# A streaming encoder trunk: the first mixer's output maps summed beforehand, and one modulation part moved into the gate

## Chip, cores and metric

The kernel runs as one launch on one core of one Trainium2 chip. The metric is the device time of that launch in microseconds (us). The engines are TensorE (PE in the rows, its weight loads PEld), VectorE (DVE), ScalarE (ACT), GpSimd (POOL) and SyncE (SP), whose queue issues most of the DMA transfers.

## What is computed

Two layers over 512 tokens of 1024 channels, in float32. The first layer is a state-space mixer (S5) with a gated linear unit behind it and then a feed-forward part; the second is an attention layer and again a feed-forward part. Each part takes a shift, a scale and a gate from the condition vector c. Cut to what the change touches:

```python
c_act = silu(c)
shift1, scale1, gate1, shift2, scale2, gate2 = split(c_act @ ada_w[0] + ada_b[0], 6)
h = rms_norm(x, norm1_g[0]) * (1 + scale1) + shift1
# S5: 64 groups of 16 channels, a complex diagonal state of 64 per group
#   state[t] = A * state[t-1] + B u[t]
#   y = Re(C state) + d * h
g = gelu(y)
x = x + gate1 * g * sigmoid(g @ w_glu + b_glu)
h = rms_norm(x, norm2_g[0]) * (1 + scale2) + shift2
x = x + gate2 * swiglu(h)
```

`ada_w[0]` is 1024 x 6144; the kernel works off its six parts of 1024 columns one by one, and names them by their place in the result: 0 and 8 (shift1, scale1), 16 (gate1), 24 (shift2), 32 (scale2), 40 (gate2).

## The kernel before, in words

**The S5 stage (`s5`).** The 512 steps are cut into 64 chunks of 8. Within a chunk the output is a product with a matrix of kernels (`intra`, L786); across chunks the state is summed per chunk (`sums`, L749), turned into a real recurrence (`turned`, L758), scanned (`scan`, L779), turned back, and multiplied by output maps (`inter`, L798). The groups are worked in quarters q = 0 to 3 for sums, turned, scan and kernels, and in eighths for inputs, intra and inter. The inputs of a quarter's products come from:

- `vmap(q)` on GpSimd (L586): three maps `vv[q][:, 0..2]`, in six products of 128x512. Re(C A^r) is map 0 plus map 1, Im(C A^r) is map 0 plus map 2. Both `kernels(q)` and `inter` multiply by the maps as they stand, so each complex product costs four matmuls, for (state part, map) = (0,0), (0,1), (1,0), (1,2).
- `tables(q)` on GpSimd (L598): the turning tables, five operations of 128x512, used by both `turned(q, False)` and `turned(q, True)`.
- `kernels(q)` (L658): products in PSUM, a copy on ScalarE (L670), a write to DRAM (`kd`, L672) and eight reads back (`tt`, L674), which spread it out for `intra`.

The maps of quarters 2 and 3 lie in part on the place of the normed input `xn`, which `inputs` (L727) reads.

**The modulation parts (`ada_rows`, L280).** A part is eight tiles of 128x1024, loaded from the SP queue (L290) into a ring of four places, of which three are the ring `raw` that the weights use later. Four *pairs* of tiles (eight matmuls each, L301) build a row sum; *close* copies the row to `adrow` on ScalarE (L306), spreads it with eight small matmuls (L309) and adds the bias. `adrow` uses the two-place ring `t1`, which is also the ring of the helper tiles `m` of `turned`. The rest of the parts, from 40 on, are worked off on VectorE much later. Each pair sends off two more loads.

**The order.** The tensor work of the S5 stage is chained by hand with `do(...)`, in the order of the calls at L825 to L891; GpSimd's work is chained by `behind(...)`. Other engines' instructions take the order that the scheduler gives them. Most products of the stage share one PSUM bank (`ps`): inputs, kernels, the closes and the transposes of the outputs (L814).

**The gate (`glu`, L1036).** gelu's output is split into a high and a low part (`split`, L920), and each weight block (128 columns of 1024 rows) is loaded, cast to its high part on ScalarE (L904) and its rest computed on VectorE (L164). Two blocks are multiplied at full width, then six at half width twice, as `outputs` (L998) says; after each half the next norm is started by `between`. `later` and `tick` (L119 to L125) put steps between matmuls by an estimated clock, in microseconds.

Of the kernel before, what the change touches and what calls it, by code (L numbers as in the profile page):

```python
# [11 lines left out]
F32 = mybir.dt.float32  # L12
# [3 lines left out]
ALU = mybir.AluOpType  # L16
# [39 lines left out]
class Trunk:  # L56
# [222 lines left out]

    def ada_rows(self, jobs, place):  # L280

# [10 lines left out]
        def pair(n, i):  # L292
            if i == 0:
                self.rows_acc = self.ps("ac")
            ks = (2 * i, 2 * i + 1)
            ws = [tiles.pop((n, k)) for k in ks]

            last = None
            for j in (3, 2, 1, 0):
                with self.after(last):  # L300
                    last = nc.tensor.matmul(self.rows_acc[32 * j:32 * j + 32], lhsT=self.csil[:, ks[j // 2]:ks[j // 2] + 1].to_broadcast([P, 32]),  # L301
                                            rhs=ws[j // 2][:, j % 2 * 512:j % 2 * 512 + 512], start=(i == 0), stop=(i == 3)).ins

        def close(at):
            row = self.tmp.tile([P, 512], F32, tag="t1", name=self.name("adrow"))
            nc.scalar.copy(out=row, in_=self.rows_acc)  # L306
            pt = self.ps()[:, 0:8]
            for m in range(4):
                nc.tensor.matmul(pt[:, 2 * m:2 * m + 2], lhsT=row[:, m * P:(m + 1) * P], rhs=self.rows, start=True, stop=True)  # L309
            cols = lambda t: t[:, at:at + 8].rearrange("a (h m) -> a m h", h=2)  # L310
            if at < 16:
                v.tensor_tensor(out=cols(self.mod), in0=pt.rearrange("a (m h) -> a m h", h=2), in1=cols(self.adab), op=ALU.add)
                return
            col = self.cst([P, 8], name="adcol")
            nc.scalar.copy(out=col, in_=pt)
            self.put_off.append(lambda: v.tensor_tensor(out=cols(self.mod), in0=col.rearrange("a (m h) -> a m h", h=2),
                                                        in1=cols(self.adab), op=ALU.add))

# [89 lines left out]
    def s5(self, ada):  # L408
# [4 lines left out]
        with ExitStack() as es:  # L413
# [172 lines left out]
            def vmap(q):  # L586
# [5 lines left out]
                return last  # L592


            turns = [[sp.tile([P, 8, 64], F32, tag=t, name=t) for t in ("tc", "ts")],
# [202 lines left out]
            def inter(q):  # L798
                for j in range(4):
                    gp = q * 4 + j  # L800
                    for n, (i, m) in enumerate(((0, 0), (0, 1), (1, 0), (1, 2))):
                        for b in range(2):
                            bp = slice(b * 64, b * 64 + 64)
                            self.last_mm = nc.tensor.matmul(py[q][bp, j * P:(j + 1) * P], lhsT=sb[q // 2 % 2][bp, i, gp % 8],  # L804
                                                            rhs=vv[gp // 8][bp, m, gp % 8].rearrange("a r p -> a (r p)"),
                                                            start=False, stop=(n == 3 and j == 3)).ins
                nc.scalar.copy(out=yt.rearrange("a i (g p) -> a g i p", p=16)[:, q % 2 * 4:q % 2 * 4 + 4],
                               in_=py[q].rearrange("a (g i p) -> a g i p", i=8, p=16))
                if q % 2:
                    ft = q // 2  # L810
# [9 lines left out]
            def behind(fn, q):  # L820
                nonlocal turn
                with wait(turn):
                    turn = fn(q)
# [9 lines left out]
            do(inputs, 3)  # L833
            pair()
            do(sums, 0)
# [5 lines left out]
            do(inputs, 5)  # L841
            pair()
            do(inputs, 6)
            pair()
            do(inputs, 7)
            do(kernels, 1)
            behind(vmap, 2)
            behind(tables, 2)
            pair()
# [4 lines left out]
            turned(0, True)  # L854
            behind(vmap, 3)
            behind(tables, 3)
            scan(1)
            do(sums, 2)
            do(inter, 0)
            pair()  # L860
            do(kernels, 2)
# [4 lines left out]
            turned(1, True)  # L866
            do(sums, 3)
            pair()
            do(inter, 2)
            scan(2)  # L870
            do(kernels, 3)
            do(intra, 3)
            pair()
# [8 lines left out]
            do(inter, 4)  # L882
            pair()
            do(inter, 5)
# [151 lines left out]
    def glu(self, between):  # L1036
# [15 lines left out]
        def blocks(m):  # L1052
            dst = [self.at(32 + 8 * m + 4 * i, [P, KT, P], F32R) for i in range(2)] if m < 2 else None
            return [self.wblock(self.io["s5_w_glu"][0], 0, KT, m * P, P, dst)]

# [512 lines left out]
    def run(self):  # L1568
        io, v, g = self.io, self.nc.vector, self.nc.gpsimd
        self.setup()  # L1570
        a0, a1, kv = io["ada_w"][0], io["ada_w"][1], io["kv_ada_w"]
        first = [(a0, at * P, at) for at in (0, 8, 16, 24, 32)]
        halves = lambda src, col, at, n: [(src, (col + 4 * i) * P, at + 4 * i, 4) for i in range(n)]
        later = halves(a0, 40, 40, 2) + halves(kv, 0, 96, 4) + halves(a1, 0, 48, 10)
        self.s5(first)
        self.banks(ps=6, st=2)
        self.wring = self.ctx.enter_context(self.tc.tile_pool(name="wring", bufs=4, reuse_waits="tile"))
        self.glu(self.ffn_in(0))
        self.dump("x1", self.xT)
# [37 lines left out]
```

## Time and profile before

| | us |
|---|---|
| median of 3 runs | 1234.67 |
| lowest, highest | 1229.35, 1234.99 |
| the profiled execution | 1233.43 |
| its span, first to last instruction | 1231.6 |
| S5 stage, up to the gate's first matmul | 175.4 |

How to read it: the profiled execution is one run, with the hardware's own record of each instruction; what is read of it below is its trace. "Busy" counts what an engine executes, "idle before" how long it had stood when an instruction began, and an arrow names who released it. PEclk (or the granted clock) is TensorE's clock as a share of its full speed. A matmul row can stand for two halves of a float32 product, so `inter`'s 32 products are 64 rows.

### The profile page before, as it was taken

To read this page: it belongs to the slowest core of one execution; us is meant where nothing else is said; L and a number is where in the kernel's file an instruction comes from. 1 tells how busy PE (TensorE), PEld (TensorE's weight loads), DVE (VectorE), ACT (ScalarE), POOL (GpSimd) and SP (SyncE) were. 2 spreads that over 40 slices of the span, in tenths; PEclk is the share of its full clock that TensorE was granted. 3 is DMA by queue.
4 is the path that set the end of the run, shared out by engine and by line. 5 is a ranking of instruction groups with operands and counts; after the bars stand their busy time and mean duration, and the time that the engine had idled before them with its cause. 6 is when DMAs were issued, how large, how long until landed. Compare 5 with 4: busy or idle time off the path is not lost.

```text
span 1231.6 us, 18830 instructions
## 1 busy us (share of the span) xinstructions
PE 1150.9 (93%) x7286; PEld 972.6 (79%) x7286; DVE 751.9 (61%) x1472; ACT 492.2 (40%) x914; POOL 133.7 (11%) x175
## 2 busy tenths in 40 slices
PE   5786879899999999999988888999999999999998
PEld 2555679888777777779987767889987888888888
DVE  8863347679788952565769899958752333232233
ACT  4641145343222232224567767834422223222222
POOL 5954000000000000000033242000000000000000
PEclk7897989899999999999998999999999999999999
DMA  9498834458878852455511121037443232323333
GB/s 273 176 258 145 180 86 139 119 147 261 258 249 259 270 172 85 134 157 155 153 41 31 35 69 35 1 92 209 137 131 100 86 103 86 102 78 103 111 115 100
DMA packets 230074, 167.53 MB, mean 136 GB/s; under 512 B 9776, under 2 KB 204256, under 8 KB 229984
## 3 DMA queue, kind: packets, MB, share of 16 engines
q1 hardware_dynamic: 208904, 128.47, 37.4%
q10 hardware_dynamic: 21080, 37.85, 9.2%
q8 instruction: 57, 0.93, 0.3%
q14 instruction: 33, 0.27, 0.1%
HBM read 163.21 MB, written 3.08 MB: 135 GB/s over the span
## 4 chain that ended last, share of the span: by engine, by line
PE 84%; DVE 8%; DMA 3%; ACT 3%; issue 1%; POOLq 0%; SPq 0%; DVEq 0%; ACTq 0%
PE ps L915 24%; PE ps L916 24%; PE ps L917 24%; PE ad L804 2%; PE ps L146 1%; PE ac L301 1%; DMA adaw<-in_ada_w 1%; DMA a<-in_x 1%; DVE a L923 1%; PE po L916 1%; PE zz L754 1%; DVE a L158 1%; DVE a L161 1%; DVE mn L1520 1%; PE po L917 1%
## 5 line engine op out<-in xcount | busy, mean ns | idle before, releaser
L916 PE MATMUL ps<-a,wh 128*128 128x512 f32 (+1 forms) x1406 | 493.7, 353 | 0.8 <-DVE a L989 0.8
L915 PE MATMUL ps<-a,wh 128*128 128x512 f32 (+1 forms) x1406 | 490.9, 354 | 3.5 <-ACT a L988 3.5
L917 PE MATMUL ps<-a,wl 128*128 128x512 f32 (+1 forms) x1406 | 494.1, 353 | 0.0
L904 ACT CAST wh<-raw 128x1024 fp32r<-128x1024 f32 (+1 forms) x179 | 182.6, 1022 | 503.7 <-PE ps L916 379.7
L164 DVE TENSOR_TENSOR wl<-raw,wh 128x1024 fp32r<-128x1024 f32 x173 | 207.1, 1199 | 193.9 <-ACT wh L904 190.2
L915 PEld LDWEIGHTS ps<-a,wh 128*128 128x128 f32 x1406 | 263.1, 189 | 44.0 <-ACT a L988 4.5
L916 PEld LDWEIGHTS ps<-a,wh 128*128 128x128 f32 x1406 | 265.4, 189 | 40.5 <-DVE a L989 1.1
L917 PEld LDWEIGHTS ps<-a,wl 128*128 128x128 f32 x1406 | 265.5, 189 | 39.6
L350 DVE SCALAR_TENSOR_TENSOR acc<-a,csil,acc 128x512 f32<-128x512 f32 x126 | 94.4, 749 | 31.0 <-DMA a<-in_ada_w 22.2
L1106 DVE TENSOR_TENSOR si<-si,ps 128x512 f32<-128x512 f32 x44 | 30.1, 684 | 81.0 <-PE ps L917 78.2
L146 PE MATMUL ps<-ident,a 128*128 128x128 f32 (+1 forms) x304 | 46.5, 295 | 17.4 <-DVE a L1447 4.8
L164 POOL TENSOR_TENSOR a<-raw,a 128x768 fp32r<-128x768 f32 (+1 forms) x2 | 4.6, 2309 | 506.3 <-ACT a L904 506.3
L146 PEld LDWEIGHTS ps<-ident,a 128*128 128x128 f32 (+1 forms) x304 | 37.4, 144 | 24.3 <-POOL a L158 6.1
L995 DVE SCALAR_TENSOR_TENSOR xT<-ps,mod,xT 128x256 f32<-128x256 f32 (+1 forms) x35 | 20.4, 582 | 45.8 <-PE ps L917 45.5
L1521 ACT ACTIVATE a<-ps,mn 128x128 f32<-128x128 f32 (+1 forms) x64 | 34.5, 546 | 13.3 <-DVE mn L1520 13.0
L915 PE MATMUL ps<-wh,a 128*128 128x288 f32 (+3 forms) x100 | 33.4, 336 | 1.8 <-ACT a L1521 1.3
L301 PE MATMUL ac<-adaw,csil 128*32 128x512 f32 x128 | 21.8, 708 | 13.7 <-DMA adaw<-in_ada_w 13.2
L916 PE MATMUL ps<-a,a 128*128 128x256 f32 (+2 forms) x108 | 33.4, 311 | 0.0
L915 PE MATMUL ps<-a,a 128*128 128x256 f32 (+2 forms) x108 | 33.1, 313 | 0.0
L917 PE MATMUL ps<-a,a 128*128 128x256 f32 (+2 forms) x108 | 32.8, 310 | 0.0
L917 PE MATMUL ps<-wh,a 128*128 128x288 f32 (+3 forms) x100 | 32.8, 329 | 0.0
L916 PE MATMUL ps<-wl,a 128*128 128x288 f32 (+3 forms) x100 | 32.6, 328 | 0.0
(317 smaller groups left out, 1473.1 us busy)
## 6 DMA issues: line engine op xcount, KB each, us to landing
a<-in_ada_w ACTq DMA_DIRECT2D x112, 256.0 KB, 4.3
raw<-in_ffn_w_gate SPq DMA_DIRECT2D x44, 512.0 KB, 3.9
raw<-in_ffn_w_up SPq DMA_DIRECT2D x44, 512.0 KB, 5.5
raw<-in_ffn_w_down SPq DMA_DIRECT2D x42, 512.0 KB, 4.2
adaw<-in_ada_w SPq DMA_DIRECT2D x32, 512.0 KB, 6.9
a<-in_kv_ada_w ACTq DMA_DIRECT2D x32, 256.0 KB, 4.3
raw<-in_ffn_w_down SPq DMA_DIRECT2D x21, 384.0 KB, 3.5
raw<-in_s_w_glu SPq DMA_DIRECT2D x14, 512.0 KB, 4.4
```

The source lines that it names most:

```text
L146: self.nc.tensor.transpose(out=out, in_=in_, identity=ident)
L164: eng.tensor_tensor(out=out, in0=a, in1=b, op=ALU.subtract)
L301: last = nc.tensor.matmul(self.rows_acc[32 * j:32 * j + 32], lhsT=self.csil[:, ks[j // 2]:ks[j // 2] + 1].to_broadcast([P, 32]), rhs=ws[j ...
L350: v.scalar_tensor_tensor(out=acc, in0=x, scalar=self.csil[:, k:k + 1], in1=acc, op0=ALU.mult, op1=ALU.add)
L804: self.last_mm = nc.tensor.matmul(py[q][bp, j * P:(j + 1) * P], lhsT=sb[q // 2 % 2][bp, i, gp % 8], rhs=vv[gp // 8][bp, m, gp % 8].rearran ...
L904: nc.scalar.copy(out=flat(wh), in_=flat(raw))
L915: mm(out, lhsT=lhs[0], rhs=rhs[0], start=start, stop=False)
L916: mm(out, lhsT=lhs[0], rhs=rhs[1], start=False, stop=False)
L917: self.last_mm = mm(out, lhsT=lhs[1], rhs=rhs[0], start=False, stop=stop).ins
L995: self.nc.vector.scalar_tensor_tensor(out=self.xT[:, m, sl], in0=src, scalar=gate[:, m:m + 1], in1=self.xT[:, m, sl], op0=ALU.mult, op1=AL ...
L1106: nc.vector.tensor_tensor(out=t, in0=t, in1=pp[i][1], op=ALU.mult)
L1521: nc.scalar.activation(out=p[:, self.OFF[t]:self.OFF[t] + w], in_=pt, func=AF.Exp, scale=-1.0, bias=mn[:, t:t + 1], accum_out=su[:, t:t + 1])
```

## The change

Three edits go together.

- `added(q)` on GpSimd: map 0 is added to maps 1 and 2 in place, in four operations of 128x512, once `kernels(q)` has read the maps. `inter` then takes two matmuls, (0,1) and (1,2), in place of four.
- The part at 32 leaves the S5 stage. Its loads and steps are put into the gate by the estimated clock: load k at 1.5 k, the pairs and the close from 13.0 on, 2.9 apart. Its tiles go to places of the arena that the S5 stage leaves. In the S5 stage five calls of `pair()` go, and the row tile of a close gets a place of its own (`sums`) in place of one of `t1`.
- Orders: GpSimd does tables 2, added 0, maps 2, maps 3, added 1, tables 3, added 2, added 3 (before: maps 2, tables 2, maps 3, tables 3). The casts of the gate's first weight block wait on ScalarE for the copy of inter 6, the others for that of inter 7, and their VectorE halves for the last operation of `turned(3, True)`.

```diff
-            row = self.tmp.tile([P, 512], F32, tag="t1", name=self.name("adrow"))
+            row = self.tmp.tile([P, 512], F32, **({"tag": "sums", "bufs": 1} if rows == "ac" else {"tag": "t1"}), name=self.name("adrow"))
...
-            if at < 16:
+            if at not in (16, 24):
...
+            def added(q):
+                for i in (1, 2):
+                    for h in (0, 4):
+                        x = vv[q][:, :, h:h + 4]
+                        last = g.tensor_tensor(out=x[:, i], in0=x[:, i], in1=x[:, 0], op=ALU.add)
+                return last
...
-                    for n, (i, m) in enumerate(((0, 0), (0, 1), (1, 0), (1, 2))):
+                    for n, (i, m) in enumerate(((0, 1), (1, 2))):
...
             do(inputs, 3)
-            pair()
             do(sums, 0)
...
-            pair()
             do(inputs, 6)
-            pair()
             do(inputs, 7)
+            behind(tables, 2)
+            behind(added, 0)
             do(kernels, 1)
             behind(vmap, 2)
-            behind(tables, 2)
+            behind(vmap, 3)
             pair()
...
             turned(0, True)
-            behind(vmap, 3)
+            behind(added, 1)
             behind(tables, 3)
             scan(1)
             do(sums, 2)
             do(inter, 0)
-            pair()
             do(kernels, 2)
...
             do(sums, 3)
+            behind(added, 2)
             pair()
             do(inter, 2)
             scan(2)
             do(kernels, 3)
+            behind(added, 3)
...
             do(inter, 4)
-            pair()
             do(inter, 5)
...
-            return [self.wblock(self.io["s5_w_glu"][0], 0, KT, m * P, P, dst)]
+            with self.tc.issue_after(self.s5_last.ins), self.tc.issue_after((self.s5_out if m else self.s5_late).ins):
+                return [self.wblock(self.io["s5_w_glu"][0], 0, KT, m * P, P, dst)]
...
-        first = [(a0, at * P, at) for at in (0, 8, 16, 24, 32)]
+        first = [(a0, at * P, at) for at in (0, 8, 16, 24)]
...
+        load, steps = self.ada_rows([(a0, 32 * P, 32)], lambda n, k: self.at(80 + 4 * k, [P, 1024]), "st", "st")
+        for k in range(KT):
+            self.later(1.5 * k, lambda k=k: load(0, k))
+        for i, f in enumerate(steps):
+            self.later(13.0 + 2.9 * i, f)
         self.glu(self.ffn_in(0))
```

## Rows read from the trace of the kernel before

**Rows 1.** The page, busy time of each engine over the whole span.
```profile
PE 1150.9 (93%) x7286; PEld 972.6 (79%) x7286; DVE 751.9 (61%) x1472; ACT 492.2 (40%) x914; POOL 133.7 (11%) x175
```
**Rows 2.** Windows: stretch, its length, busy of each engine, clock, DMA share, GB/s.
```profile
57.00:90.30 33.30, 27.78 (x415) 18.68 (x413) 21.38 (x33) 17.13 (x53) 18.53 (x16) 0.95 0.81 221
90.30:175.40 85.10, 63.44 (x965) 52.74 (x961) 34.11 (x49) 21.23 (x40) 17.12 (x14) 0.86 0.73 155
176.00:188.00 12.00, 12.00 (x61) 10.14 (x60) 2.74 (x4) 4.29 (x8) 0.00 (x0) 1.00 0.01 2
188.00:221.40 33.40, 33.34 (x282) 32.94 (x281) 26.24 (x53) 18.11 (x30) 0.00 (x0) 1.00 0.55 158
221.40:232.00 10.60, 7.54 (x39) 7.25 (x40) 10.35 (x21) 6.89 (x12) 0.00 (x0) 0.68 0.72 199
```
**Rows 3.** Matmul groups of 90.3 to 175.4: busy, mean ns, idle before.
```profile
L804 PE MATMUL ad<-a,a 64*64 64x128 f32 x512 | 30.2, 274 | 0.0
L301 PE MATMUL ac<-adaw,csil 128*32 128x512 f32 x44 | 7.8, 645 | 4.3 <-DMA adaw<-in_ada_w 4.3
L754 PE MATMUL zz<-a,a 128*64 128x64 f32 x128 | 5.8, 270 | 6.0 <-DVE a L776 6.0
L814 PE MATMUL ps<-ident,a 128*128 128x128 f32 x24 | 4.4, 311 | 9.9 <-ACT a L817 7.7 <-ACT a L807 2.2
L309 PE MATMUL ps<-rows,adrow 128*128 128x2 f32 x16 | 2.9, 304 | 0.7 <-ACT a L817 0.7
```
**Rows 4.** Timeline of TensorE in that stretch: start, length, what, idle before.
```profile
106.68 0.66 PE L814 MATMUL ps<-ident,a 128*128 128x128 f32 x4 [2.09 <-ACT a L817]
...
117.89 3.68 PE L754 MATMUL zz<-a,a 128*64 128x64 f32 x64 [6.04 <-DVE a L776]
...
145.48 1.92 PE L301 MATMUL ac<-adaw,csil 128*32 128x512 f32 x4 [4.27 <-DMA adaw<-in_ada_w]
147.33 4.40 PE L804 MATMUL ad<-a,a 64*64 64x128 f32 x64
...
162.66 1.12 PE L814 MATMUL ps<-ident,a 128*128 128x128 f32 x4 [4.91 <-ACT a L817]
```
**Rows 5.** Timeline of VectorE in the S5 stage.
```profile
64.28 2.68 DVE L161 TENSOR_TENSOR a<-a,sgu 128x512 f32<-128x512 f32 x2
...
80.38 0.68 DVE L161 TENSOR_TENSOR a<-a,sgu 128x512 f32<-128x512 f32 x1
...
87.78 0.67 DVE L164 TENSOR_TENSOR a<-zz,m 128x504 f32<-128x504 f32 x1
94.43 0.69 DVE L158 TENSOR_TENSOR m<-zz,a 128x512 f32<-128x512 f32 x1 [5.98 <-POOL a L610]
...
110.06 0.69 DVE L158 TENSOR_TENSOR m<-zz,a 128x512 f32<-128x512 f32 x1 [14.33 <-PE ps L309]
```
**Rows 6.** Timeline of ScalarE in the S5 stage.
```profile
87.32 0.61 ACT L756 COPY rr<-r 128x504 f32<-128x504 f32 x1 [3.24 <-DVE zz L781]
...
161.01 1.04 ACT L904 CAST wh<-raw 128x1024 fp32r<-128x1024 f32 x1 [3.96 <-DMA raw<-in_s_w_glu]
```
**Rows 7.** Timeline of GpSimd: an in-place add, and its last two waits and tables.
```profile
28.31 1.27 POOL L161 TENSOR_TENSOR a<-a,a 128x512 f32<-128x512 f32 x1
...
80.86 1.15 POOL L158 TENSOR_TENSOR a<-a,pw 128x512 f32<-128x512 f32 x1 [14.45 <-DMA tt<-kd]
...
106.55 1.26 POOL L610 TENSOR_TENSOR ts<-k,k 128x512 f32<-128x512 f32 x1
```
**Rows 8.** Timeline of the SP queue around kernels 1, issue times.
```profile
88.23 0.38 SPq L672 DMA_DIRECT2D kd<-a  x1
...
91.32 6.35 SPq L674 DMA_DIRECT2D a<-kd  x8
```
**Rows 9.** The line of the reads back (L674): issue to landing of one.
```profile
DMA to landing us min/median/max: 4.0/7.0/9.3
```

More of the change, by code (lines that the diff above doesn't have):

```diff
@@ L278, in vectors, with ada_rows @@
         self.kvag, self.qg = cols[:, 48:50], cols[:, 50:52]
-    def ada_rows(self, jobs, place):
+    def ada_rows(self, jobs, place, rows="ac", cols="ps"):
         nc, v = self.nc, self.nc.vector
@@ L293, in pair @@
             if i == 0:
-                self.rows_acc = self.ps("ac")
+                self.rows_acc = self.ps(rows)
             ks = (2 * i, 2 * i + 1)
@@ L304, in close @@
         def close(at):
-            row = self.tmp.tile([P, 512], F32, tag="t1", name=self.name("adrow"))
+            row = self.tmp.tile([P, 512], F32, **({"tag": "sums", "bufs": 1} if rows == "ac" else {"tag": "t1"}), name=self.name("adrow"))
             nc.scalar.copy(out=row, in_=self.rows_acc)
-            pt = self.ps()[:, 0:8]
+            pt = self.ps(cols)[:, 0:8]
             for m in range(4):
                 nc.tensor.matmul(pt[:, 2 * m:2 * m + 2], lhsT=row[:, m * P:(m + 1) * P], rhs=self.rows, start=True, stop=True)
-            cols = lambda t: t[:, at:at + 8].rearrange("a (h m) -> a m h", h=2)
-            if at < 16:
-                v.tensor_tensor(out=cols(self.mod), in0=pt.rearrange("a (m h) -> a m h", h=2), in1=cols(self.adab), op=ALU.add)
+            part = lambda t: t[:, at:at + 8].rearrange("a (h m) -> a m h", h=2)
+            if at not in (16, 24):
+                v.tensor_tensor(out=part(self.mod), in0=pt.rearrange("a (m h) -> a m h", h=2), in1=part(self.adab), op=ALU.add)
                 return
@@ L315, in close @@
             nc.scalar.copy(out=col, in_=pt)
-            self.put_off.append(lambda: v.tensor_tensor(out=cols(self.mod), in0=col.rearrange("a (m h) -> a m h", h=2),
-                                                        in1=cols(self.adab), op=ALU.add))
+            self.put_off.append(lambda: v.tensor_tensor(out=part(self.mod), in0=col.rearrange("a (m h) -> a m h", h=2),
+                                                        in1=part(self.adab), op=ALU.add))
         steps = []
@@ L805, in inter @@
                                                             rhs=vv[gp // 8][bp, m, gp % 8].rearrange("a r p -> a (r p)"),
-                                                            start=False, stop=(n == 3 and j == 3)).ins
-                nc.scalar.copy(out=yt.rearrange("a i (g p) -> a g i p", p=16)[:, q % 2 * 4:q % 2 * 4 + 4],
+                                                            start=False, stop=(n == 1 and j == 3)).ins
+                self.s5_out = nc.scalar.copy(out=yt.rearrange("a i (g p) -> a g i p", p=16)[:, q % 2 * 4:q % 2 * 4 + 4],
                                in_=py[q].rearrange("a (g i p) -> a g i p", i=8, p=16))
+                if q == 6:
+                    self.s5_late = self.s5_out
                 if q % 2:
```

## Prediction

> **What bounds the kernel now.** I read the page first: TensorE is busy 93% of the span [rows 1], so a change counts where it takes TensorE work away or lets it start sooner. Then the windows [rows 2], because an average hides the stages. From 176 us on TensorE is busy without a break at full clock (12.00 of 12.00, then 33.34 of 33.40), so what is put in there costs its whole length. In the stretch 90.3 to 175.4, the back half of the S5 stage, it is busy only 63.4 of 85.1 us at a granted clock of 0.86. That is where this change works. Then I took that stretch by groups [rows 3] to see what the busy time is made of, and by time [rows 4] to see what ends each wait. The waits in [rows 3] add up to 20.9 us (9.9, 6.0, 4.3, 0.7); 85.1 - 63.4 = 21.7 is all. Last I followed three of them on the other engines [rows 5, 6] and GpSimd's and the SP queue's own pace [rows 7 to 9].
>
> **A. From 57 to 90.3, up to sums 2.** Sums 2 needs the banks that `turned(0, True)` frees; its last operation runs at 87.78 [rows 5] and ends at 88.45, so the VectorE chain from sums 0 is the bound here and TensorE, with 27.8 of 33.3 us busy, follows. The change takes three pairs out of this stretch, one of them ahead of sums 0, which brings the chain forward by about 1 us (a pair is 7.8 us over 5.5 of them, at most 1.4, in [rows 3]); a bias add leaves VectorE. Against it: kernels 1 and its copy stay behind inputs 6 and 7 on ScalarE, and the close of part 16 now stands directly before sums 2. GpSimd now does tables 2 and added 0 here, where it stood idle for 14.45 us [rows 7], waiting really for the transposes of inputs 7, whose place maps 2 overwrite; tables 2 touch no such place.
>
> One thing speaks against more GpSimd work at this spot. The same VectorE add `a<-a,sgu`, two inputs in SBUF, took 1.34 us each at 64.28, when GpSimd was at work, and 0.68 at 80.38, when it stood idle [rows 5]. In the Trainium skill, the page "SBUF — State Buffer", section "Who interferes with whom", says that a VectorE instruction with two SBUF inputs contends with a GpSimd one that reads SBUF. The trace agrees, by that pair of rows. Here the one add of that kind left in the stretch (inputs 4) now falls beside added 0. By the pair of rows that is +0.66 us; without such contention it would be nothing. The `turned` operations take one input from PSUM. So I set sums 2 at 88.5 in place of 90.3: **-1.8** (ends -3.5, and +1.5 if ScalarE's queue delays kernels 1's copy as it does now, behind the `rr` copy that waits 3.24 us for a scan [rows 6]).
>
> **B. From sums 2 to the gate's first matmul, now 85.1 us.** Busy 63.4 [rows 2].
> - Inter: half of 512 rows, 30.2 us [rows 3], goes: -15.1.
> - One pair (7.8/5.5 = 1.4) and one close (2.9/2 = 1.45) fewer in this stretch: -2.9.
> - Half-clock losses behind waits that go. The 64 rows of sums 3 took 3.68 us behind a 6.04 us wait [rows 4] against 5.8 - 3.68 = 2.1 for those of sums 2 [rows 3]; half a pair took 1.92 against 0.7 and the inter behind it 4.40 against 30.2/8 = 3.8, behind 4.27 us; four transposes 1.12 against 0.66, behind 4.91. Together -3.9.
>
> That leaves 41.5 busy. Of the 21.7 us idle, these go:
> - 6.04 before sums 3. VectorE stood 14.33 us until 110.06 [rows 5] for a place in `t1` that the close's row held; with a place of its own that goes, and so do the 5.98 us for tables 2 at 94.43, now made before maps 2.
> - 4.27 for a row tile at 145.48: each pair now sits further behind the pair whose end sends off its loads.
> - 4.91 shrinks to the 0.75 of the other transposes: ScalarE held the gelu back behind a cast that waited 3.96 us for a weight [rows 6]; the casts now come after the last copies.
>
> So 21.7 - 14.5 = 7.2 idle stays, mostly the copy and gelu between transposes, with one table load (2.09 [rows 4]). What is late next is `tt`. From kd's issue at 88.23 [rows 8] to the last of eight reads landed it is 3.1 + 6.35 + 7.0 = 16.4 us [rows 8, 9]. After the change TensorE's own work between kernels 3 and intra 6 is intra 3 to 5, two pairs, a close, inter 3 to 5 at 1.9 and two rounds of transposes, about 17 us; for kernels 1 and intra 2 it is about the same. So this cover just holds; I add 2 us (0 to 8). GpSimd is not late. An in-place add is 1.27 us [rows 7], so `added` costs 4 x 1.27 = 5.1 and all four 20.3. From the end of tables 1 on (66.4, 14.45 before 80.86), tables 2 take it to 73.5, added 0 to 78.6, maps 2 and 3 from 80 to 92.5, added 1 to 97.6, tables 3 to 104.7, added 2 to 110, added 3 to 115 (now it ends at 107.8 [rows 7]). Inter 2, 4 and 6, which wait for added 1, 2 and 3, come up on TensorE near 105, 119 and 127, counted from 88.5 by the order of the calls and the lengths above.
> B becomes 41.5 + 7.2 + 2 = 50.7, which is **-34.4** (ends -39 and -22).
>
> **C. In the gate.** Four pairs and a close come into a stretch that is full: 4 x 1.2 (the pairs outside the slow one: (7.8 - 1.92)/5) + about 1 = 5.5 us, at most 4 x 1.4 + 1.45 = 7.1, all on the path. Their eight loads (4.2 MB) cost nothing where they fall, because the DMA share is 0.01 from 176 to 188 and 0.55 after [rows 2]; without that cover each would stand before a weight block. The casts of the first block now come late, which hides behind the last transposes, and the ring behind them starts emptier: +1.5 (0 to 8). Together **+7** (5 to 15). The steps that are chained to TensorE's estimated clock come before the first half ends, so the norm has scale2 in time.
>
> **D. Behind it.** At 221.4 to 232 TensorE is busy 7.5 of 10.6 us at clock 0.68 [rows 2], waiting for the norm while VectorE is at 10.35 of 10.6. The inserted pairs let VectorE catch up a little; the gap could shrink by up to 5 or grow by as much. I take **0**. Everything later only moves.
>
> **Sum.** -1.8 - 34.4 + 7 + 0 = -29.2. Against the profiled execution, 1233.4, that is **1204**; the median of the shown runs is 1.2 higher than that execution, well under what counts. A difference under 0.5% (6 us) can't be told from none here.
>
> **The rivals.**
> - *The round trip through DRAM becomes the bound.* For: the cover computed above equals its length; one landing can be 9.3 [rows 9]. Against: with fewer row tiles beside them the reads should land sooner. Three waits of 5 us, each with about 2 us of half clock behind it as in [rows 4], less the 2 taken: +19, **1223**.
> - *The moved loads collide in the gate.* The tiles lie where maps 2 and 3 and the output tile were, so seven of eight can't start before the last inters; if the SP queue has them ahead of the next weight blocks, TensorE waits for about two landings' worth: +12, **1216**. Against: the idle DMA time in [rows 2].
> - *Half clock.* With half of inter gone the rest is looser: behind each of the three long waits in [rows 4] the next group took up to 1.8 times its usual time, which is the lower of the clock's two levels, 1.2 and 2.4 GHz. If half of the 41.5 us runs so: +20, **1224**. The Trainium skill, "TensorE: Matmul & The Clock Gate", section "HAM oscillation", has this as a pattern of its own, work between waits that starts at half clock each time. The 0.86 of [rows 2] agrees that it happens here; against it, the longest waits are the ones that go.
> - *The S5 stage is held by its transfers, and ends when it does now.* Then A and B give nothing and C is left at its upper end, 7.1 and a couple for the ring: +9, **1242**, slower. The place is the stage's last `tt` and row tiles; it decides if their landing, and not TensorE's order, sets intra 6. For: DMA shares of 0.81 and 0.73 [rows 2]. Against: only 4.3 of 21.7 idle us end on a DMA [rows 3].
>
> **How the numbers follow.** Forecast with its own ends, 1193 to 1213: 0.65. Round trip 0.11, collision 0.11, half clock 0.07, transfers 0.04, 0.02 for smaller than all. The range 1193 to 1224 takes in the first four in most of their chance. Faster by over 0.5% (below 1228) takes all but the last and some of the large ends: 0.92; within 0.5%: 0.05; slower: 0.03.
>
> **What would show it.** Right: L804 has 256 rows at some 15 us; the gate's first matmul comes near 139; VectorE's 14.33 us wait and TensorE's 6.04, 4.27 and 4.91 are gone; the moved pairs add some 5 to 7 us between there and the norm. Wrong: intra 2 or 6 waiting for `a<-kd` (round trip), weight waits in the gate's halves (collision), a clock of 0.8 or less from sums 2 on (half clock), or GpSimd ending later than 120.

## The result, and the profile after

| | before | after |
|---|---|---|
| median (lowest to highest), us | 1234.73 (1229.35 to 1234.99) | 1201.78 (1199.19 to 1203.47) |
| profiled execution, its span | 1233.43, 1231.6 | 1201.67, 1199.9 |
| sums 2 starts | 90.35 | 87.60 |
| the gate's first matmul | 175.37 | 142.64 |
| ScalarE loads the table for silu (the feed-forward part behind the gate) | 256.64 | 228.72 |

The ratio is 0.9741 (95% interval 0.971 to 0.9773): 33 us faster. 1204 was forecast, with a range of 1193 to 1224.

The milestones in the last three rows are starts of single instructions in the two traces, and all that follows goes by them. The stage up to sums 2 gives 2.7 us, the rest of the S5 stage 30.0, the gate takes back 4.8 (81.3 us from its first matmul to silu before, 86.1 after), and what lies behind silu is 3.8 us shorter (975.0 to 971.2).

The page, busy time of each engine, against [rows 1]:

```profile
PE 1131.3 (94%) x7030; PEld 954.1 (80%) x7030; DVE 754.3 (63%) x1472; ACT 491.3 (41%) x913; POOL 154.7 (13%) x191
```

TensorE has lost the 256 rows of inter and 19.6 us, GpSimd has gained 21.0 us, of which 19.8 are `added`. The windows of after, columns as in [rows 2]: up to sums 2, the rest of the S5 stage, the gate's start, its full stretch, and the gap at the norm.

```profile
57.00:87.60 30.60, 25.54 (x390) 19.18 (x388) 21.95 (x32) 16.82 (x52) 30.05 (x24) 0.89 0.73 168
87.60:142.60 55.00, 43.67 (x688) 34.87 (x688) 28.86 (x43) 16.39 (x35) 26.11 (x22) 0.91 0.97 189
142.60:155.00 12.40, 12.40 (x63) 10.47 (x62) 5.63 (x6) 5.40 (x11) 0.00 (x0) 1.00 1.03 319
155.00:188.00 33.00, 33.00 (x280) 29.13 (x279) 26.28 (x51) 20.35 (x33) 0.00 (x0) 1.00 0.56 161
188.00:205.00 17.00, 13.78 (x91) 13.08 (x90) 14.20 (x30) 8.94 (x15) 0.00 (x0) 0.80 0.66 186
```

The second line answers the 85.10 us of [rows 2]: 55.00 long, 43.67 busy, 11.33 idle. Its DMA share has risen from 0.73 to 0.97: some 10.4 MB cross memory in it (189 GB/s over 55.0 us) where before it was 13.2 MB in 85.1 us, weights of the gate and of the moved part among them. Its matmul groups, columns as in [rows 3]:

```profile
L811 PE MATMUL ad<-a,a 64*64 64x128 f32 x256 | 16.7, 287 | 0.0
...
L301 PE MATMUL ac<-adaw,csil 128*32 128x512 f32 x32 | 5.6, 777 | 4.0 <-DMA adaw<-in_ada_w 4.0
L761 PE MATMUL zz<-a,a 128*64 128x64 f32 x128 | 4.4, 231 | 0.0
...
L823 PE MATMUL ps<-ident,a 128*128 128x128 f32 x24 | 3.9, 286 | 5.8 <-ACT a L826 3.6 <-ACT a L814 2.2
...
L823 PE MATMUL zz<-ident,a 128*128 128x128 f32 x7 | 1.0, 281 | 1.6 <-ACT a L814 1.6
```

Inter (L811) is halved; the 6.0 us before the sums (L761) are gone; of the 9.9 before the transposes (L823) the 5.8 and 1.6 that belong to copy and gelu are left. One wait of 4.0 us for a row tile is still there, at another place. TensorE's timeline says where:

```profile
100.16 1.52 PE L301 MATMUL ac<-adaw,csil 128*32 128x512 f32 x8
...
103.37 2.34 PE L761 MATMUL zz<-a,a 128*64 128x64 f32 x64
...
116.30 1.93 PE L301 MATMUL ac<-adaw,csil 128*32 128x512 f32 x8 [3.99 <-DMA adaw<-in_ada_w]
118.16 3.38 PE L811 MATMUL ad<-a,a 64*64 64x128 f32 x32
...
134.59 1.97 PE L798 MATMUL ad<-a,a 128*64 128x128 f32 x32
```

Sums 3 start at once. The pair at 116.30 waits, runs at half clock (1.93 against 1.06 of a pair at full clock), and so does inter 3 behind it (3.38 against 1.96 of the inter at 89.62); the granted clock is 0.50 from 116.30 to 118. The SP queue of the same moments, issue times:

```profile
100.87 4.62 SPq L681 DMA_DIRECT2D a<-kd  x8
105.59 2.72 SPq L290 DMA_DIRECT2D adaw<-in_ada_w  x4
111.71 0.38 SPq L679 DMA_DIRECT2D kd<-a  x1
...
119.57 7.04 SPq L681 DMA_DIRECT2D a<-kd  x8
```

That pair's loads are the first two of the `adaw` ones at 105.59. Their places came free when the pair at 100.16 ended, at 101.68. By then the queue was in the eight reads of `tt` 2, which themselves had waited until 100.87 for their write to land, so the loads stood there for 3.9 us. The second of them, sent at 106.08, is the one that ends the wait, 10.2 us later; the median of the loads of L290 between 80 and 135 us is 7.5. So the wait is in part the queue's and in part the transfer's own.

### The profile page after: what moved, and what is told of

Its sections match the earlier page's. It is cut to its first block, busy times and chain, and to the rows that moved or that the text cites. A ratio compares the mean times of both kernels' runs of the same rounds, so it can differ in the third digit from the quotient of the medians.

```text
span 1199.9 us, 18340 instructions
## 1 busy us (share of the span) xinstructions
PE 1131.3 (94%) x7030; PEld 954.1 (80%) x7030; DVE 754.3 (63%) x1472; ACT 491.3 (41%) x913; POOL 154.7 (13%) x191
## 3 DMA queue, kind: packets, MB, share of 16 engines
HBM read 163.21 MB, written 3.08 MB: 139 GB/s over the span
## 4 chain that ended last, share of the span: by engine, by line
PE 84%; DVE 9%; ACT 3%; DMA 3%; issue 1%; POOL 0%; SPq 0%; ACTq 0%; DVEq 0%
PE ps L923 24%; PE ps L924 24%; PE ps L925 24%; PE ps L146 2%; DMA a<-in_x 1%; PE ad L811 1%; DVE a L161 1%; DMA adaw<-in_ada_w 1%; PE ac L301 1%; DVE a L158 1%; PE po L924 1%; ACT a L930 1%; PE po L925 1%; DVE a L931 1%; DVE mn L1529 1%
## 5 line engine op out<-in xcount | busy, mean ns | idle before, releaser
L1529 DVE TENSOR_REDUCE mn<-ps 128x1 f32<-128x128 f32 (+1 forms) x64 | 30.2, 482 | 4.6 <-PE ps L1527 4.5
```

The source lines that it names most:

```text
L1529: v.tensor_reduce(out=mn[:, t:t + 1], in_=pt, axis=AX.X, op=ALU.min)
```

## Experiments

Beside these kernels the one before was timed again, with medians of 1233.1 to 1233.7 against 1234.73 above, so their medians can be set beside 1201.78 to within about 1.5 us.

**Summed maps alone** (before with `added` and two products, nothing else):

```diff
+            def added(q): ...   # as in the change
-                    for n, (i, m) in enumerate(((0, 0), (0, 1), (1, 0), (1, 2))):
+                    for n, (i, m) in enumerate(((0, 1), (1, 2))):
             do(kernels, 1)
+            behind(added, 0)
             behind(vmap, 2)
...
             behind(vmap, 3)
+            behind(added, 1)
...
```

> The kernel before with the summed maps alone: added(0) ahead of maps 2 in GpSimd's idle time, added 1 to 3 behind maps 3, maps 3 and kernels 3; part 32, the row tile in t1 and the casts as before. Theory of the prediction (inter's 30.2 us lie on TensorE's path, so half of them is 15.1): 1234.7 - 15 = about 1220. Rival (the waits of the old order, 6.0 for t1, 4.3 for a row tile, 4.9 for a cast, end at times that other queues set, so that they grow when inter shrinks): 6 to 9 us gained, 1226 to 1229.

Measured 1219.07 (1218.19 to 1222.84), ratio 0.9886 (0.9858 to 0.9914): the theory's number. Alone, the maps give 14.6 us, and the wait of [rows 4] before sums 3 stays, as its timeline of TensorE shows; a close at 141.80 now waits 6.78 us as well:

```profile
112.80 3.69 PE L761 MATMUL zz<-a,a 128*64 128x64 f32 x64 [6.78 <-DVE a L783]
```

**Everything but the summed maps** (after with four products and no `added`):

```diff
-                    for n, (i, m) in enumerate(((0, 1), (1, 2))):
+                    for n, (i, m) in enumerate(((0, 0), (0, 1), (1, 0), (1, 2))):
-            behind(added, 0)   # and added 1 to 3
```

> The changed kernel with four products in inter and no added; all else as changed. Theory of the prediction: 15.1 us come back, 1217. Rival: in the new order part of that work would fill the 4 us wait for a row tile at 116 and the half clock behind it (about 2 us), so 8 to 10 us come back, 1210 to 1212.

Measured 1213.45 (1211.06 to 1214.41), ratio 0.9832 (0.9807 to 0.9857): the maps are worth 11.7 us here, between the two expectations. Its window from sums 2 to the gate, and the pair that waits in after:

```profile
87.70:150.20 62.50, 55.43 (x945) 46.64 (x946) 28.92 (x43) 16.65 (x35) 8.14 (x7) 0.97 0.87 167
...
118.32 1.06 PE L301 MATMUL ac<-adaw,csil 128*32 128x512 f32 x8 [0.39 <-DMA adaw<-in_ada_w]
```

The maps take 11.8 us of busy time out of this window (55.43 - 43.67), not 15.1, and 4.3 us of that come back as idle time (11.33 against 7.07): TensorE comes to that row tile at 117.9 and waits 0.39 us, where in after it comes at 112.3 and waits 3.99. The granted clock is 0.97 here and 0.91 in after. So part of what the halved products free is spent waiting for a transfer, and part goes to the lower clock, most of it behind that wait.

**The part at 32 left in the S5 stage** (after with the five calls of `pair()` back, and no steps in the gate):

```diff
-        first = [(a0, at * P, at) for at in (0, 8, 16, 24)]
+        first = [(a0, at * P, at) for at in (0, 8, 16, 24, 32)]
...
             do(inputs, 3)
+            pair()
             do(sums, 0)
...
             do(inter, 4)
+            pair()
             do(inter, 5)
...
```

> The changed kernel with part 32 back in the S5 stage (the five pair() calls as before), not in the gate. Theory of the prediction (three pairs out of the stretch to 90.3 gave 1.8, one pair and a close 2.9, the row tile wait with its half clock about 5.5, against 7 in the gate, measured 5.2): 3 to 5 us slower, 1205 to 1207. Rival (tensor work only moved from one full stretch to another): no difference, 1200 to 1203.

Measured 1211.66 (1210.42 to 1212.85), ratio 0.982 (0.9795 to 0.9845): 9.9 us slower than after, more than either theory. TensorE's timeline of it, then its SP queue:

```profile
133.44 1.92 PE L301 MATMUL ac<-adaw,csil 128*32 128x512 f32 x4 [8.56 <-DMA adaw<-in_ada_w]
```

```profile
119.77 5.08 SPq L681 DMA_DIRECT2D a<-kd  x8
124.95 0.39 SPq L290 DMA_DIRECT2D adaw<-in_ada_w  x1
```

Again a row tile stands behind eight reads back, here those of `tt` 3, and TensorE waits 8.56 us for it. The gate starts 9.5 us later and is 5.8 us shorter without the moved steps, and what lies behind silu is 5.2 us longer. The move is thus worth 9.5 us in the S5 stage, where I had given it about 1 us of work ahead of sums 2 and 2.9 behind, and the 4.27 us wait.

**The part left out altogether.** Its scale is the bias alone; four pairs, a close and eight loads are missing:

```diff
...
-        for i, f in enumerate(steps):
-            self.later(13.0 + 2.9 * i, f)
+        v.tensor_copy(out=self.mod[:, 32:40], in_=self.adab[:, 32:40])
```

> The changed kernel with part 32's loads, pairs and close left out of the gate; scale2 is then the bias alone, so the output is not the reference's. Theory of the prediction (what is put into the gate costs its whole length): 5.2 us less, 1196.5. Rival (the pairs fill time that TensorE would spend waiting at the norm behind the gate, where VectorE is the one that is full): 0 to 2 us less, 1200 to 1202.

Measured 1195.31 (1192.3 to 1195.75), ratio 0.9697 (0.9671 to 0.9723): 6.5 us less than after, somewhat more than the theory's 5.2. In the traces the gate, from its first matmul to silu, is 6.2 us shorter (79.9 against 86.1). That is what the moved part costs where it now stands.

**The casts of the gate's weights without their order:**

```diff
-            with self.tc.issue_after(self.s5_last.ins), self.tc.issue_after((self.s5_out if m else self.s5_late).ins):
-                return [self.wblock(self.io["s5_w_glu"][0], 0, KT, m * P, P, dst)]
+            return [self.wblock(self.io["s5_w_glu"][0], 0, KT, m * P, P, dst)]
```

> The changed kernel without the order on the gate's weight casts. Theory of the prediction: the gelu stands behind a cast that waits for a weight again, 4.2 us of idle and about 1.4 us of half clock: 1207. Rival (with part 32's last tiles gone from the ring the weights come early enough, and the order costs nothing or gains nothing): 1200 to 1203.

Measured 1212.02 (1211.51 to 1214.53), ratio 0.983 (0.9801 to 0.9859): 10.2 us, about twice what the theory had. ScalarE's timeline of it, then TensorE's:

```profile
135.88 1.04 ACT L912 CAST wh<-raw 128x1024 fp32r<-128x1024 f32 x1 [8.97 <-DMA raw<-in_s_w_glu]
136.83 0.58 ACT L814 COPY a<-ad 128x512 f32<-128x512 f32 x1
```

```profile
139.10 1.11 PE L823 MATMUL ps<-ident,a 128*128 128x128 f32 x4 [8.75 <-ACT a L814]
...
151.35 1.97 PE L823 MATMUL zz<-ident,a 128*128 128x128 f32 x8 [2.72 <-ACT a L814]
```

It is the mechanism of [rows 6], in a larger size: ScalarE stands 8.97 us before a cast whose weight hasn't landed, and the copy of inter's output, for which TensorE waits, is queued behind it. Before, the same wait was 3.96 and TensorE's 4.91. TensorE comes to this place 27.4 us sooner than before (139.10 - 8.75 against 162.66 - 4.91), the weight only 25.1 (135.88 against 161.01); a second wait of 2.72 and half clock behind both (1.97 against 1.09 for the last transposes in after) make the rest. So the order is worth more after the other edits than its row of before suggested; on before it was not tried alone.

**The row tile of a close back in `t1`:**

```diff
-            row = self.tmp.tile([P, 512], F32, **({"tag": "sums", "bufs": 1} if rows == "ac" else {"tag": "t1"}), name=self.name("adrow"))
+            row = self.tmp.tile([P, 512], F32, tag="t1", name=self.name("adrow"))
```

> The changed kernel with the close's row tile back in the ring t1. Theory of the prediction (the row's place in t1 made VectorE's 14.3 us wait and TensorE's 6.0 before sums 3): some 6 to 8 us come back, 1208 to 1210. Rival (the close now stands close behind its last pair, so the row holds its place for under 2 us, and the place of the close, not of the row, took the wait away): 0 to 1 us, 1201 to 1203.

Measured 1209.1 (1208.32 to 1210.81), ratio 0.9815 (0.9785 to 0.9845): 7.3 us, as the theory had it, but not at its place. VectorE waits for the close that now stands before sums 2, as its timeline and then TensorE's show:

```profile
89.79 0.69 DVE L158 TENSOR_TENSOR m<-zz,ts 128x512 f32<-128x512 f32 x1 [4.70 <-PE ps L309]
```

```profile
91.80 3.68 PE L761 MATMUL zz<-a,a 128*64 128x64 f32 x64 [2.12 <-DVE a L783]
```

The close has moved from before sums 3 to before sums 2, and the collision with `turned` moved with it; sums 3 don't wait in this kernel. Not all of the 7.3 us can be placed. Sums 2 come 1.7 to 2.0 us later than in the three kernels that ran at the same clock up to there (89.80 to 90.11, see A below), and they and the inter behind them run at half clock (3.68 against 2.08, 3.08 against 1.96), together 4.4 to 4.7 us.

**Tables 2 behind maps 2 on GpSimd:**

```diff
-            behind(tables, 2)
             behind(added, 0)
...
             behind(vmap, 2)
+            behind(tables, 2)
             behind(vmap, 3)
```

> The changed kernel with tables 2 behind maps 2 again on GpSimd (added 0, maps 2, tables 2, maps 3, then as changed). Theory of the prediction (the 6.0 us that VectorE stood for tables 2 was part of the way to sums 3): tables 2 end near 88, before or just as VectorE has turned(2, False) to do at 89.8, so at most 1 us. Rival (any delay of GpSimd goes through added 1 and tables 3 to TensorE): 3 us or more.

Measured 1202.83 (1201.41 to 1205.61), ratio 0.9766 (0.9739 to 0.9793): within 1.1 us of after, as expected. VectorE's wait of 5.98 us for tables 2 [rows 5] doesn't come back. It waits 8.53 us for tables 3 instead, at 110.01, and TensorE, which stands for a row tile at that time anyway, hardly loses by it.

**Is the row tile's wait of 3.99 us worth its length?** The pair at 100.16, whose end sends off the late loads, is put before kernels 2, so that these loads stand in the queue ahead of the write and the reads of kernels 2:

```diff
             do(inter, 0)
+            pair()
             do(kernels, 2)
             do(inter, 1)
-            pair()
```

> The changed kernel with the first pair of part 24 back between inter 0 and kernels 2, so that the loads it sends off stand in the SP queue ahead of kd 2 and tt 2. Theory from the trace of the changed kernel (the 4.0 us wait at 116 is a load that stood behind the eight reads of tt 2): that wait and the half clock behind it, 0.9 + 1.4 us, go: 1195.5. Rival (the reads of tt 2 or tt 3 are then what is late): 0 to 2 us less, 1200 to 1202.

Measured 1202.3 (1198.76 to 1203.7), ratio 0.9755 (0.9727 to 0.9783): nothing gained, the rival's time. The row tile waits are gone; TensorE's timeline shows two others in their place, for `tt` (the second, though its row names no releaser, counts among the waits for the reads, 4.1 us in both):

```profile
103.08 1.71 PE L798 MATMUL ad<-a,a 128*64 128x128 f32 x16 [1.39 <-DMA a<-kd]
104.50 3.12 PE L761 MATMUL zz<-a,a 128*64 128x64 f32 x64
...
133.64 3.26 PE L798 MATMUL ad<-a,a 128*64 128x128 f32 x32 [2.67 <-issue]
```

Its SP queue:

```profile
114.98 0.33 SPq L290 DMA_DIRECT2D a<-in_ada_w  x1
115.40 1.48 SPq L679 DMA_DIRECT2D kd<-a  x1
```

The load at 114.98 is one of the moved part's. It stands before the write of kernels 3 and waits for its own place in the arena. Is that what holds the write, or is the round trip itself the bound? Three more kernels, all with the pair early. The first orders the moved part's loads behind the last read of `tt` 3:

```diff
...
+        def behind_tt(k):
+            with self.tc.issue_after(self.tt_last):
+                load(0, k)
...
-            self.later(1.5 * k, lambda k=k: load(0, k))
+            self.later(1.5 * k, lambda k=k: behind_tt(k))
```

> pair_early (the pair of modulation parts between the third and the fourth kernel's positions, so that its weights have time to land) with one order added: the loads of the moved part's weights, which the gate reads, go out on SyncE behind the last read-back of the fourth maps. Theory, that what pair_early gained was lost because one of those loads stood in SyncE's queue waiting for its place ahead of the fourth write: the fourth write goes out some 3 us earlier, the 2.67 us in front of the last products (133.64 in pair_early) and most of the half-clock loss behind it go, the gate starts at 138.5 to 139.5 instead of 142.6 to 143.0, and the time is 1197 to 1198.5 us. Rival, that the round trip through memory itself, write and eight reads, is the bound whatever stands ahead of it: the gate starts at 142 to 143 and the time is 1200 to 1202.5 us.

Measured 1198.24 (1197.03 to 1203.68), ratio 0.9726 (0.9706 to 0.9745): the theory's time, but in the profiled execution, which is the longest of the four, the rival's gate, at 143.86. Its SP queue, then TensorE:

```profile
115.21 0.38 SPq L679 DMA_DIRECT2D kd<-a  x1
```

```profile
105.75 3.46 PE L761 MATMUL zz<-a,a 128*64 128x64 f32 x64
...
134.09 3.68 PE L798 MATMUL ad<-a,a 128*64 128x128 f32 x32 [2.15 <-DMA a<-kd]
```

Of these 143.86, some 2 us were lost before sums 2, which come at 90.11 here and at 88.20 in the kernel with the early pair alone; the cause of that is not the queue (see A below).

The second has two orders more: the gate's own weights behind the same read, and on ScalarE the `rr` copies, which feed the scan, behind the copy that the write of the kernels takes (L677).

```diff
+                with wait(self.k_out) if q > 1 else ExitStack():
                     nc.scalar.copy(out=rr[q % 2][:, :, 1:64], in_=r8[:, q * 8:q * 8 + 8].unsqueeze(2).to_broadcast([P, 8, 63]))
...
+            with self.tc.issue_after(self.tt_last), self.tc.issue_after(self.s5_last.ins), ...
```

> queue_clear with two more orders: the gate's other weights go out on SyncE behind the same read-back, and on ScalarE the copies of the filter positions stand behind the copy that completes the maps of the kernel before, so that the second write isn't held by them. Theory: the second write goes some 2 us earlier, the 1.39 us in front of the third products (103.08 in pair_early) goes too, the gate starts at 136.5 to 138.5 and the time is 1195 to 1197.5 us. Rival, that the round trip is the bound: gate at 142 to 143, 1200 to 1202.5 us. If the gate's own weights then come late, its first product waits, and the time is above queue_clear's.

Measured 1198.44 (1196.96 to 1201.95), ratio 0.9723 (0.9707 to 0.9739), with the gate at 140.11: between the two. Its SP queue, then TensorE:

```profile
110.47 0.79 SPq L679 DMA_DIRECT2D kd<-a  x1
...
118.70 4.78 SPq L681 DMA_DIRECT2D a<-kd  x8
```

```profile
102.43 2.03 PE L761 MATMUL zz<-a,a 128*64 128x64 f32 x64
...
130.41 3.63 PE L799 MATMUL ad<-a,a 128*64 128x128 f32 x32 [2.15 <-DMA a<-kd]
```

The third has the order on ScalarE alone.

> pair_early with the order on ScalarE alone (the copies of the filter positions behind the copy that completes the maps), SyncE's queue left as it is. Theory: only the 1.39 us in front of the third products goes, the 2.67 us in front of the last ones stay, since the load that waits for its place still stands ahead of the fourth write; gate at 141 to 142, 1199 to 1201 us. Rival, that the waits on SyncE's queue don't matter: the same time as queue_clear_rr, within 1 us.

Measured 1202.48 (1198.58 to 1202.53), ratio 0.9741 (0.9728 to 0.9755). That is above the theory's 1199 to 1201 and 4 us from the rival's, so neither holds in the time; the gate, at 142.42, is near the theory's. The 1.39 us wait is gone, and TensorE waits longer for `tt` 3:

```profile
132.48 3.68 PE L799 MATMUL ad<-a,a 128*64 128x128 f32 x32 [3.38 <-DMA a<-kd]
```

From the end of sums 3 to the write of kernels 3 it is 115.40 - 107.62 = 7.8 us in the kernel with the early pair alone, and 7.8 in the one with ScalarE's order; 115.21 - 109.21 = 6.0 and 110.47 - 104.46 = 6.0 where the loads stand behind the reads. The copy that the write takes ends 1.8 us ahead of the write in the first two and less than 0.1 in the others. So the load that waits for its place does hold the write, by 1.8 us; the 3 us of my expectation were too much. The wait before the last `intra` stays at 2.15 all the same: from the write's issue to those products it is 18.2 us in the first of the four (133.64 - 115.40), 18.9 in the one with ScalarE's order, and 18.9 and 19.9 where the write goes sooner. Both theories were half right. The queue's order costs 1.8 us, and behind it the round trip itself is longer than the work that covers it. From sums 2 to the gate, which leaves out what the traces differ by before, it is 55.0 us in after, 54.8 with the early pair, 53.8 and 52.0 with the loads ordered, and 54.6 with ScalarE's order alone. ScalarE's order alone gives nothing that can be seen in the time.

The two kernels with the loads ordered have medians 3.5 and 3.3 us below after's, but their intervals overlap with its own, and two of the eight times are above 1201.78. That they beat it is likely and not shown.

## Why the prediction was right, point by point

| | forecast | measured |
|---|---|---|
| A, up to sums 2 | -1.8 | -2.7 |
| B, sums 2 to the gate | -34.4 | -30.0 |
| C, in the gate | +7 | +4.8 |
| D and all behind | 0 | -3.8 |
| sum | -29.2 | -31.7 |

The bound was read rightly: B is where the time went. Of the signs named as right, the waits are gone and the moved steps cost what they should; L811 has its 256 rows at 16.7 us instead of 15, and the gate's first matmul comes at 142.64 instead of near 139. Of the signs named as wrong none shows in after: GpSimd ends at 114.2 (115 was set), TensorE's clock from sums 2 on is 0.91, and no product waits for `tt` or for the gate's weights. That the sum came out only 2.5 us off is luck: B's shortfall of 4.4 is offset by 6.9 from the other terms, of which 3.8 lie in a stretch where nothing was forecast and 1.6 or more of A's do not come from the change.

**A.** Sums 2 come at 87.60 (88.5 was forecast). The last operation of `turned(0, True)` ends at 86.3, 2.1 us sooner than before, and the chain is no longer the only bound: the close that now stands before sums 2 waits for its row and runs up to them, as the prediction had warned. TensorE's timeline of after:

```profile
86.62 1.05 PE L309 MATMUL ps<-rows,adrow 128*128 128x2 f32 x8 [0.65 <-ACT adrow L306]
87.60 2.08 PE L761 MATMUL zz<-a,a 128*64 128x64 f32 x64
```

Most of the 2.7 us is not the change's, though. From 59.9 us on the two kernels run the same instructions for a while, and in the trace of before they run at half clock, in that of after at full clock. TensorE's timelines, first before, then after:

```profile
59.92 1.88 PE L301 MATMUL ac<-adaw,csil 128*32 128x512 f32 x8 [0.54 <-PE ps L719]
```

```profile
59.88 1.07 PE L301 MATMUL ac<-adaw,csil 128*32 128x512 f32 x8 [0.53 <-PE ps L726]
```

From 60 to 62 the granted clock is 0.51 in before and 1.00 in after, and the write of kernels 0 goes out at 67.60 and 65.94. Of the 13 kernels of this document six have that write at 67.5 to 67.7 in their traces and seven at 65.6 to 65.9, and the change doesn't decide which: the kernel with the part left out, whose S5 stage is after's, has the loss and its sums 2 at 89.91; the summed maps alone, with before's order, don't have it, and sums 2 at 88.73. With the same clock, then, the change brings sums 2 forward by 0.4 us (90.35 to 89.91) or 1.1 (88.73 to 87.60), where 1.8 was forecast. What decides the clock there, no run shows.

The contention on which this term had a sentence shows in rows that start together, VectorE's and GpSimd's timelines of after:

```profile
78.88 1.64 DVE L161 TENSOR_TENSOR a<-a,sgu 128x512 f32<-128x512 f32 x1
```

```profile
78.88 1.09 POOL L158 TENSOR_TENSOR a<-a,pw 128x512 f32<-128x512 f32 x1
79.93 1.55 POOL L158 TENSOR_TENSOR a<-a,pw_s 128x512 f32<-128x512 f32 x1
```

The add takes 1.64 us, against 0.68 in [rows 5] with GpSimd idle: +0.96 where +0.66 was set. GpSimd's next product takes 1.55 against its usual 1.10. The section of the Trainium skill that the prediction drew on ("SBUF — State Buffer", "Who interferes with whom") says more than I used: the shared ports are an exclusive lock, and the order of issue decides which of the two engines is blocked. These rows fit a lock: VectorE loses 0.96, about the length of GpSimd's 1.09, and then GpSimd loses 0.45 while VectorE finishes at 80.52. Both start at 78.88, so they don't show which issued first.

**B.** The waits that were to go went: 6.04 before sums 3, the 4.27 at its old place, and 4.91, whose transposes now wait 0.75; copy and gelu leave 5.8 + 1.6 = 7.4 us of idle time where 7.2 was set. That the `t1` collision and the casts were real causes is shown by the two kernels that put them back (+7.3, +10.2); both are worth more than their rows of before, 6.04 and 4.91. The first puts the collision before sums 2 and says nothing of the 6.04 before sums 3. For these there is the kernel with the part left in the S5 stage: a close stands before sums 3 in it as it did before (at 101.56), its row in its own place and tables 2 early, and sums 3 start at once:

```profile
105.12 2.99 PE L761 MATMUL zz<-a,a 128*64 128x64 f32 x64
```

With the summed maps alone, the row in `t1` and tables 2 late, they wait 6.78. So the two edits together took that wait away; their shares in it are not measured apart. Two things fell short. First, inter gave 13.5 us of busy time (30.2 to 16.7), not 15.1, and the whole window 19.8 instead of 21.9, because the clock was 0.91 in it: 1.93 for a pair and 3.38 for an inter at half clock behind the row tile, and before that 1.52 for the pair at 100.16 and 1.98 for the products behind it (1.06 and 1.09 at full clock), which come behind the table load's wait. The rival on the clock was there, behind two waits instead of everywhere. Second, and this is the step that failed: "each pair now sits further behind the pair whose end sends off its loads". It does, but the loads did not go out when the pair ended. They stood in the SP queue behind the reads of `tt` 2, and the wait came back as 3.99 us at 116.30. The prediction reckoned a load's start from the pair that frees its place, and left out what stands before the load in its own queue.

The 2 us that I added for the round trip were not needed in after, because the row tile's wait covers it; the kernel that removes that wait shows the round trip directly behind (2.67 us). Its length was set too short, at 16.4, and from one of three cases: the write of kernels 1, after which the reads start 3.1 us later [rows 8]. The same queue of before had a second case, which I had not read:

```profile
101.12 0.38 SPq L672 DMA_DIRECT2D kd<-a  x1
108.53 3.76 SPq L674 DMA_DIRECT2D a<-kd  x8
```

7.4 us. In after it is 7.9 for kernels 3 (111.71 to 119.57; two weight loads stand between until 119.26, and the queue then waits 0.3 us more for the write), and the kernels above have 18.2 to 19.9 us from the write to the products. The argument that the reads would land sooner "with fewer row tiles beside them" came true for the reads (for kernels 1 to 3 a median of 7.0 us from issue to landing, 8.1 before) and left out the write ahead of them: for kernels 3 the reads start 7.9 us behind it, 2.3 before.

**C.** The moved steps, groups of the gate's stretch in after:

```profile
L301 PE MATMUL st<-a,csil 128*32 128x512 f32 x32 | 4.3, 604 | 0.0
...
L309 PE MATMUL st<-rows,adrow 128*128 128x2 f32 x8 | 0.9, 240 | 0.0
```

4.3 + 0.9 = 5.2 us of work (5.5 forecast), no wait before any of it, and no collision of the loads with the weight blocks that TensorE felt: ScalarE's casts wait 3.83 and 2.53 us for weights near 150, but TensorE is busy without a break. Leaving the part out gives 6.2 in the gate, so about 1 us lies around the work. The 1.5 us for the late casts did not show: the gate is 4.8 us longer, not 7. Left in the S5 stage the part costs 9.9 us more in all, so moving it pays although the gate is full: it trades a transfer that nothing covers for work.

**D.** The gap at the norm is as before (TensorE idle for 3.1 us in [rows 2], 3.2 after). Behind silu the kernel is 3.8 us shorter, which no step forecast. It is shorter in every kernel that has the moved part in the gate or not at all (969.7 to 972.0 us from silu to the end, against 971.2 in after), and not in the two that have it in the S5 stage (974.0 with the summed maps alone, 976.4 with the rest of the change). So it hangs on that part's place. Which instruction later on profits was not found; it stays open.

**The parts are not additive.** Taken out of after one at a time, maps, part, casts, row and tables cost 11.7, 9.9, 10.2, 7.3 and 1.1 us, together 40.2, for a change of 33. Alone on before, the maps gave 14.6.

## What to carry to other kernels

A wait for a transfer has two lengths: that of the transfer, and that of what stands before it in its issuing queue, where a load whose place is not yet free or a read whose write has not landed holds everything behind it; follow the issue time as well as the landing. When an edit makes the compute shorter, look at which transfers keep their time, because they become the next waits, and price an order that hides them by the stage after the edit and not before it. In a stage full of such waits, moving work to a stretch that is busy without a break can pay, since there it costs little more than its own length. And before a milestone of one trace is set against that of another, look whether what both do ahead of it ran at the same clock.

## What the runs showed of the hardware

The write of 240 KB to DRAM has no fixed time to landing: its reads, which wait for it, start 3.1, 7.4 and 2.3 us after it in before (kernels 1 to 3), 3.1, 6.1 and 7.9 in after. What the same queue sends just ahead of it matters. For kernels 2 the eight reads of the quarter before go out directly ahead in after; the kernel with the early pair, which differs by the place of that pair alone, sends two row tiles (from 95.78 on) in between. Their SP queues, first after, then the early pair:

```profile
94.73 0.38 SPq L679 DMA_DIRECT2D kd<-a  x1
```

```profile
98.22 0.38 SPq L679 DMA_DIRECT2D kd<-a  x1
...
106.06 3.89 SPq L681 DMA_DIRECT2D a<-kd  x8
```

6.1 us (94.73 to 100.87) become 7.8. The other kernels agree: 7.4 to 8.4 us in all seven that send two or three row tiles just ahead of this write, 5.3 to 6.5 in the four with the reads directly ahead, and 4.4 and 6.7 in the two where a single load of the moved part goes ahead. It is one write of four, and it goes out at other times in these kernels, so this is a pattern and not a law.

The same VectorE addition took 0.68 us where GpSimd was idle as it began and 1.64 beside a busy one, at the cost of 0.45 us on the other side. And the same instructions from 60 us on ran at half clock in one trace and at full clock in another (0.51 in before, 1.00 in after, from 60 to 62), which moved the write of kernels 0 behind them by 1.7 us.
